# RWKV and GDN elementwise steps moved from VectorE to ScalarE in a one-core hybrid block

## The chip, the cores and the metric

The kernel runs on one core of a Trainium2 chip (TensorE, VectorE, ScalarE, GpSimd, the SyncE queue and 16 DMA engines). The metric is the device time of one execution in microseconds; the time of a kernel is the median of its runs. In the profile the engines are PE (TensorE's matmuls), PEld (its weight loads), DVE (VectorE), ACT (ScalarE), POOL (GpSimd) and SP (SyncE).

## The reference

One layer of a diffusion backbone, on 256 latent tokens and 256 context tokens of width 2048, all in float32. Each token is normalised and modulated, projected by `w_in`, and the result is cut into four head groups of width 512: GLA, Gated DeltaNet (GDN), a short gated convolution and RWKV-7. The outputs are concatenated, projected by `w_out` and added to the stream; then a SwiGLU of width 5632 and a last norm follow. The two recurrences that the change touches are:

```
GDN, per head, chunked:   S <- a (I - beta k k^T) S + beta k v^T,   o = S^T q
RWKV-7, per head, step:   S <- S (diag(w) - kk (a kk)^T) + v k^T,   y = S r
```

Every recurrent mixer runs forward and backward. The context tokens are processed first and only for their final states; each latent scan starts from the context state of its own direction.

## The kernel before

Channels lie on the 128 partitions and tokens on the free axis. Weights come from HBM in tiles `wraw` of 128x512; each is split into a high part `wh` (a copy to fp32r on ACT) and a low part `wl` (the difference, on DVE), and a product is made of three fp32r matmuls (`big` in the mixing part, `acc` elsewhere). The parts in order of time are: the modulation vectors and the first projections; the mixing part, in which projections, RWKV, GDN and GLA of context and latent tokens are interleaved; the output projection; the SwiGLU.

In the mixing part two streams run side by side. Stream "a" is RWKV (`rwkv(p, s)`: head pair p of 4, s = 0 for context and 1 for latent tokens, two directions d each), and stream "b" is GDN (`gdn(h, s)`: head h of 4, both directions and both halves of the tokens together) and GLA. The accumulation tiles of the streams lie in PSUM under the tags `ea` and `eb` (short use) and `la` and `lb` (the chains); `ea` and `big` have two buffers, the others one. Each of the pieces is traced in three parts, `front`, `mid` and `back`. The order of the pieces is written out in `ORDER`, with an offset of priority for many of them; the order of the instructions on each engine's queue is then drawn up when the program is built, from these priorities and a planner's costs of the instructions, and each engine works through its queue in that order. Loads and splits of weights have high priority.

RWKV: `front` computes `rw_BK` (two blocks of 128x256) and the tile `bdLM`, from which `small_inverses` starts its long row of small DVE steps. `mid` writes the blocks of `rw_BK` into block-diagonal tiles NB and KB (`halves`, four copies of 64x256; names `bd<-rw_BK`), and the same of v into VB on ACT; then four PE products with tiles `bd` are evicted as `rw_vt`, `rw_kt`, `rw_na` and `rw_ka`. `back` ends in a chain over four chunks: PE makes the new state and the output in one PSUM tile `la`; `rw_S` is the state, scaled by a column, and `rw_y` the output (copied on ACT for d = 0, added on DVE for d = 1).

GDN: `front` copies the product k k^T out of PSUM (`gd_kq`, line 1145) and `mid`, for latent tokens, k q^T (line 1179). In `back`, for each direction and half, PE makes `lb`, from which ACT writes `gd_Fb` (scaled by beta) and DVE writes `gd_Fg` (scaled by another column). `gd_Fg` is the stationary operand of the next product `eb`. `gd_Fb` and `gd_Fg` of one direction read the same PSUM tile, and the context tokens need 128 columns of it, the latent ones 256.

Of the kernel before, what the change touches and what calls it, by code (L numbers as in the profile page):

```python
# [175 lines left out]
def block_kernel(ctx: ExitStack, tc: tile.TileContext, x, cx, ada_first, ada_later, ada_b, w_in, w_early, w_out,  # L176
                 w_gu, w_down, final_g, consts, params, small, out):
    nc = tc.nc
    V, A, G, TE = nc.vector, nc.scalar, nc.gpsimd, nc.tensor
# [210 lines left out]
    with ExitStack() as st:  # L390
# [74 lines left out]
        w = early_weights(0)  # L465
# [50 lines left out]
    with mix:  # L516
# [382 lines left out]
        def rwkv(p, s, raw, sm):  # L899
# [52 lines left out]
            def mid(d, v):  # L952
                cur[0] = "a"
                lo = 1 if d == 0 else 0
                KK, BK = v["KK"], v["BK"]
                NB, KB, VB = (r.next() for r in bd[1:])
                vv = t1("rw_v")
                shift(vv, com["v"], d * 12 + 8 + p, d)
                halves(NB, BK[:, :, 0, :], V)
                halves(KB, BK[:, :, 1, :], V)  # L960
                halves(VB, c64(vv), A)
                if s == 1:
                    r = t1("rw_r")
                    shift(r, com["r"], d * 12 + p, d)
                    IR = v["IR"] = mk(mx, [P, 4, 2, 64], "rw_IR", 1)
                    G.tensor_copy(IR[:, :, 0, :], bcast(istack, 1, 4))
                    tt(IR[:, :, 1, :], c64(r), v["ep"][:, :, lo:lo + 64], MUL)
                    rk = t1("rw_sq")
                    stt(rk, r, pc("rk", p), v["kp"], MUL, MUL)
                    pr = PB([P, T])  # L970
                    mm(pr, onesbd, rk)
                    if d == 0:
                        com["bonus"] = t1("rw_bonus")
                        tt(com["bonus"], pr, vv, MUL)
                    else:
                        tt(rk, pr, vv, MUL)
                        tt(com["bonus"], com["bonus"], rk, ADD, e=G)

                pv = PB([P, 4, P])
                for c in range(4):  # L980
                    TE.transpose(pv[:, c], f2(VB[:, c]), ident)
                v["vt"] = mk(mx, [P, 4, P], "rw_vt", 1)
                acopy(v["vt"], pv)

                pk = PB([P, 4, P])
                for c in range(4):
                    TE.transpose(pk[:, c], f2(KK[:, c]), ident)
                v["kt"] = mk(mx, [P, 4, P], "rw_kt", 1)
                acopy(v["kt"], pk)


                for t, tag in ((NB, "rw_na"), (KB, "rw_ka")):
                    pt, o = PB([P, 4, P]), mk(mx, [P, 4, P], tag, 1)
                    for c in range(4):
                        if s == 1:
                            mm(pt[:, c], f2(t[:, c]), f2(v["IR"][:, c]))
                        else:
                            TE.transpose(pt[:, c], f2(t[:, c]), ident)
                    if s == 1:
                        tt(o, pt, bcast(caus[d], 1, 4), MUL)  # L1000
                    else:
                        for hh in range(2):
                            sl = slice(64 * hh, 64 * hh + 64)
                            acopy(o[sl, :, :64], pt[sl, :, sl])
                    v[tag] = o

            def back(d, v):
                cur[0] = "a"
                w = P if s == 1 else 64
                LM, na, ka, kt_, vt = v["LM"], v["rw_na"], v["rw_ka"], v["kt"], v["vt"]  # L1010
                KH, EB = bdKh.next(), bdE.next()
                if s == 1 and d == 0:
                    com["y"] = t1("rw_y")
                F = mk(mx, [P, 4, P], "rw_F", 1)
                inverse(v["nL"], v["Xc"], (16, 32), [d == 0] * 4, na[:, :, :w], F[:, :, :w], w)
                pka = PB([P, 4, w], "l")
                for c in range(4):
                    mm(pka[:, c], LM[:, c, 1].rearrange("p h j -> p (h j)"), F[:, c, :w])
                for hh in range(2):
                    sl = slice(64 * hh, 64 * hh + 64)  # L1020
                    tt(KH[sl, :, hh, :], pka[sl, :, 0:64], ka[sl, :, 0:64], ADD)
                if s == 1:
                    Ah = mk(mx, [P, 4, 64], "rw_Ah", 1)
                    tt(Ah, pka[:, :, 64:P], ka[:, :, 64:P], ADD)
                pe = PB([P, 4, w], "l")
                for c in range(4):
                    mm(pe[:, c], kt_[:, c], F[:, c, :w])
                for hh in range(2):
                    sl = slice(64 * hh, 64 * hh + 64)
                    tt(EB[sl, :, hh, :], pe[sl, :, 0:64], bcast(istack[sl], 1, 4), ADD)  # L1030
                if s == 1:
                    Q = mk(mx, [P, 4, 64], "rw_Q", 1)
                    tt(Q, pe[:, :, 64:P], v["IR"][:, :, 1, :], ADD)
                S = get_state(("rw", p, d), f"rw_S{d}") if s == 1 else None
                order = (0, 1, 2, 3) if d == 0 else (3, 2, 1, 0)
                yc = c64(com["y"]) if s == 1 else None
                for n, c in enumerate(order):

                    pc_ = PB([P, 64 + P], "l")
                    po, pS = pc_[:, :64], pc_[:, 64:]  # L1040
                    if n < 3 or s == 0:
                        mm(pS, f2(KH[:, c]), vt[:, c], True, S is None)
                        if S is not None:
                            mm(pS, f2(EB[:, c]), S, False, True)
                    if s == 1:
                        mm(po, vt[:, c], Ah[:, c], True, False)
                        mm(po, S, Q[:, c], False, True)
                    if n < 3 or s == 0:
                        S = mk(mx, [P, P], f"rw_S{d}", 2)
                        ts(S, pS, v["dcol"][:, c:c + 1], MUL)  # L1050
                    if s == 1 and d == 0:
                        acopy(yc[:, c], po)
                    elif s == 1:
                        tt(yc[:, c], yc[:, c], po, ADD)
                if s == 0:
                    put_state(("rw", p, d), S)
                elif d == 1:
                    finale()
# [23 lines left out]
            for d in range(2):  # L1082
                v = {}
# [13 lines left out]
        def gdn(h, s, raw, sm):  # L1097
# [29 lines left out]
            def front():  # L1127
                cur[0] = "b"
                com.update(raw())
                k = cvs(com["k"], 1, "gd_k")  # L1130
                v = cvs(com["v"], 2, "gd_v")
                l2(k, 1.0)
                tok = mk(mx, [P, 4, P], "gd_tok", 2)
                pt = PB([P, 4, P])
                for c in range(2):
                    TE.transpose(pt[:, c], k[:, c * P:(c + 1) * P], ident)
                    TE.transpose(pt[:, 2 + c], v[:, c * P:(c + 1) * P], ident)
                acopy(tok, pt)
                pk = PB([P, 2, P])
                for c in range(2):  # L1140
                    sl = slice(c * P, (c + 1) * P)
                    mm(pk[:, c], k[:, sl], k[:, sl])
                kq = mk(mx, [P, 4, P], "gd_kq", 1)
                kk = kq[:, 0:2]
                V.tensor_copy(kk, pk)

                pbc = decays()
                dl = mk(mx, [P, 4, P], "gd_dl", 2)
                for d in range(2):
                    for c in range(2):  # L1150
                        cs = sm["cum"][:, d, h, c:c + 1]
                        V.scalar_tensor_tensor(out=dl[:, d * 2 + c], in0=pbc[:, d, c * P:(c + 1) * P], scalar=cs,
                                               in1=dlm[d], op0=SUB, op1=SUB)
                act(dl, dl, AF.Exp, scale=-1.0)
                for d in range(2):
                    for c in range(2):
                        u = d * 2 + c
                        stt(dl[:, u], kk[:, c], sm["nb"][:, d, h, c:c + 1], dl[:, u], MUL, MUL)
                com.update(kq=kq, kn=k, tok=tok, nL=dl, Xc=small_inverses(dl, lowers))

            def mid():
# [14 lines left out]
                    sl = slice(c * P, (c + 1) * P)  # L1176
                    mm(pk[:, c], k[:, sl], q[:, sl])
                kq = com["kq"][:, 2:4]
                V.tensor_copy(kq, pk)
                pbc = decays()  # L1180
                for d in range(2):
                    for c in range(2):
# [9 lines left out]
            def back():  # L1192
# [7 lines left out]
                for d in range(2):  # L1200
# [5 lines left out]
                    for c in range(2):  # L1206
                        u = d * 2 + c
                        src = pf[:, c].rearrange("p a b -> p (a b)")[:, :w]
                        acopy(Fb[:, u].rearrange("p a b -> p (a b)")[:, :w], src, scale=sm["beta"][:, d, h, c:c + 1])
                        ts(Fg[:, u].rearrange("p a b -> p (a b)")[:, :w], src, sm["nbe"][:, d, h, c:c + 1], MUL)  # L1210
                    pe = PB([P, 2, 2, P])
                    for c in range(2):
                        u = d * 2 + c
# [467 lines left out]
```

## Time and profile before

| quantity | value |
|---|---|
| median of 3 runs (lowest, highest) | 1978.37 us (1975.06, 1981.58) |
| the profiled execution's own time | 1979.17 us |
| its span, first to last instruction | 1977.4 us |
| mean granted TensorE clock | 0.983 |
| PE busy in the span | 1858.0 us (94%) |
| PEld busy | 1622.9 us (82%) |
| DVE busy | 1352.5 us (68%) |
| ACT busy | 1020.7 us (52%) |
| POOL busy | 155.0 us (8%) |

The shares are averages over parts with different limits. The mixing part goes from about 160 to 1096 us of the span, and only there do the changed lines run.

### The profile page before, as it was taken

What the parts mean: (1) busy time and instruction counts of PE and PEld (TensorE: products, weight loads), DVE (VectorE), ACT (ScalarE), POOL (GpSimd) and SP (SyncE); (2) the same over time, 40 slices, a digit from 0 to 9 for tenths busy, and PEclk for the clock granted to TensorE, in tenths of its full rate; (3) what the DMA queues carried; (4) which work ended last, traced back from release to release, by engine and by line L of the source; (5) the groups of instructions that cost most, each with busy time, mean ns of one, the idle gap of its engine ahead of it and who ended that gap; (6) DMA issues with size and microseconds to landing.
All of it is one profiled execution on the core that took longest, in us unless ns stands there. A gap on an engine that the chain in (4) does not pass through costs nothing.

```text
span 1977.4 us, 36172 instructions
## 1 busy us (share of the span) xinstructions
PE 1858.0 (94%) x13312; PEld 1622.9 (82%) x13312; DVE 1352.5 (68%) x3327; ACT 1020.7 (52%) x2125; POOL 155.0 (8%) x207
## 2 busy tenths in 40 slices
PE   5898899899999999999999998999999999999998
PEld 3777788788888988888999986888888888888886
DVE  3446767888879789899767567986555555555554
ACT  2225555575575655656455555555555545544444
POOL 0001000000001001101010001110010010000000
PEclk6999999899999999999999999999999999999999
DMA  8985877255473431322344665996555555665664
GB/s 332 397 341 199 277 244 238 69 190 176 126 240 106 146 100 61 101 72 86 110 142 143 220 185 173 318 316 212 184 189 184 189 185 187 201 207 193 193 196 153
DMA packets 162081, 374.66 MB, mean 189 GB/s; under 512 B 17896, under 2 KB 43752, under 8 KB 156784
## 3 DMA queue, kind: packets, MB, share of 16 engines
q1 hardware_dynamic: 156288, 368.21, 55.7%
q10 hardware_dynamic: 5616, 4.14, 0.7%
q8 instruction: 104, 1.70, 0.3%
q14 instruction: 73, 0.60, 0.1%
HBM read 360.48 MB, written 11.80 MB: 188 GB/s over the span
## 4 chain that ended last, share of the span: by engine, by line
PE 75%; DVE 9%; DMA 8%; ACT 5%; issue 2%; POOL 0%; SPq 0%; ACTq 0%; DVEq 0%; POOLq 0%
PE acc L214 40%; PE big L214 14%; PE la L214 6%; DMA wraw<-in_ada_later 5%; PE ea L214 5%; PE lb L214 3%; DVE wl L202 3%; PE eb L214 3%; PE ob L214 2%; ACT wh L197 2%; PE pt L214 0%; DMA wraw<-in_x 0%; DMA xin<-in_cx 0%; ACT rw_z L193 0%; DMA wraw<-in_w_in 0%
## 5 line engine op out<-in xcount | busy, mean ns | idle before, releaser
L202 DVE TENSOR_TENSOR wl<-wraw,wh 128x512 fp32r<-128x512 f32 x856 | 570.7, 693 | 370.0 <-ACT wh L197 364.0
L197 ACT ACTIVATE wh<-wraw 128x512 fp32r<-128x512 f32 x856 | 509.9, 625 | 485.9 <-PE acc L214 197.0
L214 PE MATMUL acc<-n,wh 128*128 128x512 f32 x1408 | 492.7, 398 | 3.3 <-ACT wh L197 3.3
L214 PE MATMUL acc<-n,wl 128*128 128x256 f32 x1408 | 383.2, 282 | 1.8 <-DVE wl L202 1.8
L214 PE MATMUL big<-nh,wh 128*128 128x256 f32 x1056 | 311.9, 296 | 4.4 <-ACT xs L197 3.0
L214 PE MATMUL big<-nh,wl 128*128 128x256 f32 x1056 | 311.2, 295 | 0.7 <-DVE wl L202 0.7
L214 PEld LDWEIGHTS acc<-n,wh 128*128 128x128 f32 x1408 | 259.4, 189 | 60.1 <-ACT wh L197 3.6
L214 PE MATMUL big<-nl,wh 128*128 128x256 f32 x1056 | 307.7, 292 | 0.0
L214 PEld LDWEIGHTS acc<-n,wl 128*128 128x128 f32 x1408 | 267.1, 190 | 11.7 <-DVE wl L202 3.3
L214 PEld LDWEIGHTS big<-nh,wh 128*128 128x128 f32 x1056 | 200.9, 190 | 11.3 <-ACT xs L197 3.8
L214 PEld LDWEIGHTS big<-nh,wl 128*128 128x128 f32 x1056 | 200.5, 190 | 4.0 <-issue 2.1
L214 PEld LDWEIGHTS big<-nl,wh 128*128 128x128 f32 x1056 | 200.8, 190 | 2.0 <-issue 1.1
L214 PE MATMUL acc<-wh,hH 128*128 128x512 f32 x352 | 137.6, 391 | 0.0
L214 PE MATMUL acc<-wh,hL 128*128 128x512 f32 x352 | 137.2, 390 | 0.0
L214 PE MATMUL acc<-wl,hH 128*128 128x512 f32 x352 | 137.2, 390 | 0.0
L202 POOL TENSOR_TENSOR hL<-sg,hH 128x256 fp32r<-128x256 f32 x44 | 46.7, 1061 | 452.5 <-ACT hH L197 452.5
L214 PEld LDWEIGHTS acc<-wh,hH 128*128 128x128 f32 x352 | 66.1, 188 | 14.1 <-ACT up L197 0.2
L214 PEld LDWEIGHTS acc<-wl,hH 128*128 128x128 f32 x352 | 66.1, 188 | 13.9 <-DVE wl L202 0.2
L214 PEld LDWEIGHTS acc<-wh,hL 128*128 128x128 f32 x352 | 66.1, 188 | 13.8
L214 PE MATMUL ob<-wraw,sc 128*32 128x128 f32 x1536 | 52.7, 280 | 24.9 <-DMA wraw<-in_ada_later 21.2
L214 PEld LDWEIGHTS ob<-wraw,sc 128*32 128x32 f32 x1536 | 39.9, 111 | 34.2 <-DMA wraw<-in_ada_later 27.6
L202 DVE TENSOR_TENSOR wl<-wr,wh 128x1408 fp32r<-128x1408 f32 x16 | 26.0, 1624 | 43.3 <-ACT wh L197 43.3
(482 smaller groups left out, 3175.3 us busy)
## 6 DMA issues: line engine op xcount, KB each, us to landing
wraw<-in_w_gu SPq DMA_DIRECT2D x174, 512.0 KB, 3.3
wraw<-in_w_in SPq DMA_DIRECT2D x264, 256.0 KB, 3.2
wraw<-in_ada_later SPq DMA_DIRECT2D x256, 256.0 KB, 4.2
wraw<-in_w_down SPq DMA_DIRECT2D x88, 512.0 KB, 4.2
ad<-in_ada_first SPq DMA_DIRECT2D x32, 1024.0 KB, 9.8
wraw<-in_w_out SPq DMA_DIRECT2D x64, 256.0 KB, 2.8
wr<-in_w_early SPq DMA_DIRECT2D x16, 704.0 KB, 6.2
xin<-in_cx SPq DMA_DIRECT2D x2, 1024.0 KB, 7.9
```

Of the source, the lines that this page charges most:

```text
L197: A.activation(o, i, AF.Copy)
L202: (e or V).tensor_tensor(out=o, in0=a, in1=b, op=op)
L214: return TE.matmul(o, l, r, start=start, stop=stop)
```

## The change

Five sets of instructions keep their operands and results and change their engine, from DVE to ACT: RWKV's copies into NB and KB, its chunk states `rw_S`, GDN's two copies out of PSUM, and its products `gd_Fg`. `V.tensor_copy` and `ts` run on DVE; `acopy` is an ACT activation "Copy", with a scale if one is given.

```diff
@@ rwkv, mid
-                halves(NB, BK[:, :, 0, :], V)
-                halves(KB, BK[:, :, 1, :], V)
+                halves(NB, BK[:, :, 0, :], A)
+                halves(KB, BK[:, :, 1, :], A)
                 halves(VB, c64(vv), A)
@@ rwkv, back
                         S = mk(mx, [P, P], f"rw_S{d}", 2)
-                        ts(S, pS, v["dcol"][:, c:c + 1], MUL)
+                        acopy(S, pS, scale=v["dcol"][:, c:c + 1])
@@ gdn, front
-                V.tensor_copy(kk, pk)
+                acopy(kk, pk)
@@ gdn, mid
-                V.tensor_copy(kq, pk)
+                acopy(kq, pk)
@@ gdn, back
                         acopy(Fb[:, u].rearrange("p a b -> p (a b)")[:, :w], src, scale=sm["beta"][:, d, h, c:c + 1])
-                        ts(Fg[:, u].rearrange("p a b -> p (a b)")[:, :w], src, sm["nbe"][:, d, h, c:c + 1], MUL)
+                        acopy(Fg[:, u].rearrange("p a b -> p (a b)")[:, :w], src, scale=sm["nbe"][:, d, h, c:c + 1])
```

## Rows read from the trace of the kernel before

**Rows 1.** Busy time by stretch (us, instructions), granted clock, DMA share, GB/s.

```profile
core 0: us, PE busy (x) PEld busy (x) DVE busy (x) ACT busy (x) POOL busy (x), PEclk, DMA share, GB/s
...
160.00:360.00 200.00, 173.74 (x1928) 154.04 (x1928) 142.02 (x445) 113.61 (x261) 18.47 (x37) 0.98 0.75 242
360.00:960.00 600.00, 566.09 (x4729) 515.73 (x4729) 521.30 (x1658) 355.93 (x796) 52.09 (x82) 0.99 0.38 121
960.00:1096.00 136.00, 131.46 (x1022) 124.24 (x1022) 91.72 (x204) 72.98 (x159) 13.94 (x14) 1.00 0.46 146
```

**Rows 2.** What PE waited for, 360 to 960 us: total, times, longest.

```profile
PE ob L214 <- DMA wraw<-in_ada_later: 6.5, 7, 1.9
PE ea L214 <- DVE rw_BK L202: 3.9, 4, 1.3
PE eb L214 <- DVE gd_Fg L206: 3.0, 4, 1.4
...
PE ea L998 <- ACT rw_na L197: 1.8, 3, 1.2
...
PE la L214 <- DVE rw_Ah L202: 0.2, 1, 0.2
PE la L214 <- ACT ivaX L197: 0.2, 1, 0.2
```

**Rows 3.** Groups on DVE by shape: count, busy us, mean ns, idle before.

```profile
L206 DVE TENSOR_SCALAR rw_S<-la,rw_dcol 128x128 f32<-128x128 f32 x56 | 19.4, 347 | 9.3 <-PE la L214 8.8
...
L873 DVE COPY bd<-rw_BK 64x256 f32<-64x256 f32 x64 | 18.4, 287 | 1.4 <-PE ea L998 0.6
...
L206 DVE TENSOR_SCALAR gd_Fg<-lb,gnbe 128x256 f32<-128x256 f32 x16 | 7.7, 480 | 2.3 <-ACT gd_Fb L199 2.1
...
L206 DVE TENSOR_SCALAR gd_Fg<-lb,gnbe 128x128 f32<-128x128 f32 x16 | 5.5, 345 | 1.4 <-ACT gd_Fb L199 1.4
...
L1145 DVE COPY gd_kq<-eb 128x256 f32<-128x256 f32 x8 | 3.4, 419 | 0.4 <-PE eb L214 0.3
```

**Rows 4.** Groups on ACT of the nearest shapes.

```profile
L197 ACT ACTIVATE xs<-big 128x256 f32<-128x256 f32 x56 | 20.2, 371 | 0.9 <-PE big L214 0.7
...
L197 ACT ACTIVATE bd<-rw_v 64x256 f32<-64x256 f32 x32 | 13.2, 412 | 2.2 <-PE ea L981 1.6 <-DVE rw_v L211 0.2
...
L199 ACT ACTIVATE gd_Fb<-lb,gbeta 128x256 f32<-128x256 f32 x16 | 7.5, 472 | 11.3 <-PE lb L214 9.7 <-DVE gd_Fg L206 1.5
...
L199 ACT ACTIVATE gd_Fb<-lb,gbeta 128x128 f32<-128x128 f32 x16 | 5.8, 361 | 3.2 <-PE lb L214 2.3 <-DVE gd_Fg L206 0.8
```

**Rows 5.** DVE busy on rw_S, 360 to 960 us.

```profile
360.00:960.00 600.00, 15.58 (x45) 0.99 0.38 121
```

**Rows 6.** DVE busy on line 873, 360 to 960 us.

```profile
360.00:960.00 600.00, 14.37 (x50) 0.99 0.38 121
```

**Rows 7.** DVE busy on gd_Fg, 360 to 960 us.

```profile
360.00:960.00 600.00, 9.90 (x24) 0.99 0.38 121
```

**Rows 8.** Timeline of DVE: start, us, instruction.

```profile
735.40 0.28 DVE L873 COPY bd<-rw_BK 64x256 f32<-64x256 f32 x1
735.60 1.40 DVE L202 TENSOR_TENSOR bdLM<-ea,consts 64x512 f32<-64x512 f32 x2
736.92 0.89 DVE L873 COPY bd<-rw_BK 64x256 f32<-64x256 f32 x3
...
738.34 0.69 DVE L202 TENSOR_TENSOR ivaXT<-la,rw_na 128x512 f32<-128x512 f32 x1
```

**Rows 9.** Timeline of PE: the first product that reads those copies.

```profile
748.81 1.11 PE L214 MATMUL ea<-rw_IR,bd 128*128 128x128 f32 x8
```

**Rows 10.** Timeline, 952 to 957 us: one direction of GDN's products.

```profile
952.19 0.47 ACT L199 ACTIVATE gd_Fb<-lb,gbeta 128x256 f32<-128x256 f32 x1 [1.22 <-PE lb L214]
952.69 0.48 DVE L206 TENSOR_SCALAR gd_Fg<-lb,gnbe 128x256 f32<-128x256 f32 x1
953.21 0.47 ACT L199 ACTIVATE gd_Fb<-lb,gbeta 128x256 f32<-128x256 f32 x1 [0.55 <-DVE gd_Fg L206]
...
953.72 0.48 DVE L206 TENSOR_SCALAR gd_Fg<-lb,gnbe 128x256 f32<-128x256 f32 x1 [0.54 <-ACT gd_Fb L199]
```

**Rows 11.** What ACT waited for, 360 to 960 us, longest first.

```profile
ACT wh L197 <- PE big L214: 36.4, 41, 2.8
```

**Rows 12.** What DVE waited for, 360 to 960 us, longest first.

```profile
DVE wl L202 <- ACT wh L197: 10.2, 20, 1.5
```

## Prediction

> **What bounds the kernel now.** I read the table of busy shares first. PE is busy for 94% of the span, so a change of elementwise work can only act through what PE still waits for, and all changed lines lie in the mixing part. I therefore read the busy time of three stretches of that part [rows 1]. From 160 to 360 us PE is idle for 200 - 173.7 = 26.3 us; from 360 to 960 us for 600 - 566.1 = 33.9 us; from 960 to 1096 us for 136 - 131.5 = 4.5 us. That is 64.7 us in all, and no rearrangement can give back more. The middle stretch is the one to look at: there DVE is busy for 521.3 of 600 us (86.9%) and ACT for 355.9 us (59.3%). In the first stretch DVE is at 71% and the DMA engines at 75% of their time, so I expect little from DVE there.
>
> Next I read what PE waited for in the middle stretch [rows 2]. The list has 24 lines and names 32.2 of the 33.9 us. One line of 6.5 us is DMA. Sixteen lines are DVE: the first is 3.9 us, the last 0.2 us, and they sum to 19.1 us. Seven are ACT: from 1.8 us down to 0.2 us, sum 6.6 us. So the stalls that DVE ends are three times those that ACT ends. PE is the bound, with DVE close behind.
>
> **The change part by part.** Each moved instruction has its price on DVE in its own row [rows 3], and its price on ACT in that of an ACT instruction of the same shape and the same kind of source [rows 4].
>
> *Off DVE:* 56 states, 19.4 us; 64 block copies, 18.4 us; 32 `gd_Fg`, 7.7 + 5.5 = 13.2 us; eight copies of line 1145, 3.4 us; four of line 1179, which have the same shape, at 419 ns, 1.7 us. Sum 56.1 us.
>
> *Onto ACT:* the states are priced as `gd_Fb` of 128x128 (also scaled by a column, also out of PSUM): 56 x 361 ns = 20.2 us. The block copies are priced as ACT's own copies into the third of these tiles, `bd<-rw_v`: 64 x 412 ns = 26.4 us. `gd_Fg` is priced as its twin `gd_Fb`: 16 x 472 + 16 x 361 ns = 13.3 us. The 12 copies out of PSUM are priced as `xs<-big`: 12 x 371 ns = 4.5 us. Sum 64.4 us. The sources of the block copies are strided here and not in the row; the other rows of 256 columns bound it by 371 and 472 ns, 23.7 to 30.2 us, and I keep 412 since the destination is the same.
>
> So the engines' work grows by 8.3 us, nearly all of it from the block copies (287 ns on DVE against 412 on ACT). The Trainium skill ("Perfetto Trace Analysis", section "Optimizing Scalar/DVE Operations") says that an operation for which DVE has a fast mode is quicker there, and that offloading to ACT may make sense if DVE is saturated. By it the block copies should stay, and without them the sums would be 37.7 us off DVE and 38.0 us onto ACT.
>
> In the middle stretch the moved work is 15.6 us of states, 14.4 us of block copies and 9.9 us of `gd_Fg` [rows 5 to 7], 39.9 us together, and most of the 5.1 us of small copies; I take 43 us. DVE falls to 478 of 600 us (79.7%). ACT gains 43 x 64.4 / 56.1 = 49 us and rises to 405 us (67.6%).
>
> *What a lighter DVE is worth.* One place shows it [rows 8]: of four block copies in DVE's queue one stands ahead of `bdLM` and three, 0.89 us, stand ahead of `ivaXT` at 738.34 us, which PE needs. The first product that reads them starts at 748.81 us [rows 9], more than 10 us after the last ends. The copies themselves are therefore hidden behind the rest of the stream, and stay so on ACT unless they come more than 10 us later; what they cost now is the place that they take in the queue. How much of the 19.1 us of stalls goes away with 43 us less in that queue no row shows, so I bound it. If stalls go with busy time, it is 19.1 x 43/521 = 1.6 us less, and on the side of ACT 6.6 x 49/356 = 0.9 us more: net gain 0.7 us. If they go as in a queue, with u/(1-u) of the busy share u, DVE's factor falls from 6.63 to 3.93 (to 59%) and ACT's rises from 1.46 to 2.09 (to 143%): 7.8 us less and 2.8 us more, net gain 5.0 us. I take 3 us, between them.
>
> *The GDN pair.* `gd_Fb` and `gd_Fg` of one direction never overlap [rows 10]: ACT and DVE take turns on one PSUM tile, four turns from 952.19 to 954.20 us, though the four durations sum to 1.90 us, and each turn waits for the other engine's queue. On one engine the turns need no handover, so the four ACT products can take about 4 x 0.47 = 1.88 us. I give this 1 us of the 3.0 us that PE lost to `gd_Fg` [rows 2]; the bounds are 0 (if other ACT work is put between) and 3.0 us.
>
> *The states.* In a forward chunk `rw_S` and `rw_y` now follow one another on ACT and lose a handover between engines; in a backward chunk `rw_y` stays on DVE and gains one. There are as many of one kind as of the other, and `rw_S` costs 14 ns more on ACT, 56 x 14 ns = 0.8 us. I cost this at nothing; what hides it is the `big` matmuls that PE has between chunks, and without them it is 0.8 us.
>
> *Who queues behind.* Behind every moved instruction on ACT stand the copies `wh`, then DVE's `wl` and PE's projections. ACT sat idle 36.4 us before `wh`, in 41 places, because PE had not yet released a buffer [rows 11], so `wh` is mostly early; but DVE already waits 10.2 us for it, 20 times [rows 12]. That is cover for delays of some tenths of a microsecond each, not for all 49 us.
>
> Sum: 3 + 1 = 4 us less. The profiled execution took 1979.2 us, 0.8 us more than the median of the runs; so 1975.2 on its scale and 1974.4 as a median. I predict 1974.5 us.
>
> **The rivals.**
>
> *DVE sets the pace of the middle stretch.* DVE's 521.3 us is more than the weight loads' 515.7 us [rows 1], and work that PE needs queues behind copies that nobody needs yet. If so, nearly all of DVE's 19.1 us goes; ACT's share comes back a little. Price 15 us: 1963.5 us, and 1959 with all 19.1. Against it: PE at 94% leaves no more, and DMA and ACT own 13.1 us of the idle time. The Trainium skill ("Perfetto Trace Analysis", section "Identifying the Most-Contended Engine") would rate DVE as the engine to relieve, since it judges PE by its weight loads; by that rule this rival would be the forecast.
>
> *ACT comes late in RWKV's `mid` (slower).* Four copies of 412 ns, 1.65 us, now stand in ACT's queue near `rw_vt`, `rw_kt`, `rw_na` and `rw_ka`, whose evictions free the two `ea` buffers; PE already waited there for `rw_na` [rows 2]. There are 64/4 = 16 such places: 26.4 us if none is covered. With half uncovered it is 13 us, less 4 us gained: +9 us, 1987.5 us. It decides once the stalls that ACT ends grow by over 10 us. Against it: the 10 us of slack of the copies, which allows them to be queued after the evictions.
>
> *The queues are drawn up anew and fit less well.* New durations and engines change the order of every queue in the mixing part. No row prices it. The nearest are the idle shares of PE in the stretches, 13% in the first, 5.7% in the second and 3.3% in the third [rows 1]: one point more in 600 us is 6 us, and a third of the way from 5.7 to 13% is +14 us, 1992 us. It may as well go the other way by half of that.
>
> *Nothing moves:* what PE waits for is the length of the chains, and a freed DVE only waits longer. 1978 us.
>
> **How the numbers follow.** Chances: forecast 0.43 (its own range, from the bounds, 1969 to 1980 us); DVE sets the pace 0.22; ACT late 0.17; queues fit less well 0.13; nothing moves 0.05. The runs of before spread over 0.33%, so 0.3% (5.9 us) is what can be told from no change: faster is below 1972.4 us, slower above 1984.3. Faster: the second case, 0.22, and the lower third of the first, 0.14, give 0.36. Slower: 0.17 and 0.13, 0.30. Same: 0.34. The range has to reach both the DVE case, whose bound is 1959 us, and a poor order of the queues: 1958 to 1995 us.
>
> **What would show it.** DVE's busy time should fall from 1352.5 to about 1296 us and ACT's rise from 1020.7 to about 1085 us, with PE's at about 1858. PE's stalls that DVE ends should fall from 19 to about 14 us in the stretch that answers to 360 to 960 us, and those of ACT rise from 7 to about 9. `gd_Fb` and `gd_Fg` should stand four in a row on ACT. I am wrong on the gain if PE's idle time in that stretch stays at 34 us, and wrong on the sign if stalls behind `wh`, `rw_kt` or `rw_na` grow by more than 10 us, or if PE's stalls turn up at lines that the change doesn't touch.

## The result and the profile after

The change makes the kernel slower: 1987.56 us against 1974.46 us, medians of 11 runs each, taken in turn on one chip; the ratio is 1.0055, with a 95% interval of 1.0039 to 1.0071. The forecast was 4 us less. It started from 1978.37 us, the median of three runs; with eleven runs the kernel before has 1974.46 us, so it is the step of -4 us, and not the number 1974.5, that the result answers. The time lies inside the range given, on the other side of "no change".

The first view of the profile after is the busy time by stretch, in the columns of [rows 1].

```profile
160.00:360.00 200.00, 172.47 (x1910) 152.72 (x1910) 129.85 (x409) 119.91 (x283) 18.47 (x37) 0.97 0.75 241
360.00:960.00 600.00, 565.61 (x4708) 510.34 (x4709) 493.02 (x1537) 401.94 (x931) 56.68 (x86) 1.00 0.38 120
960.00:1096.00 136.00, 130.27 (x1000) 123.18 (x999) 88.69 (x190) 73.92 (x164) 11.44 (x10) 0.99 0.44 140
```

The work did change sides: in the middle stretch DVE fell from 521.3 to 493.0 us and ACT rose from 355.9 to 401.9 us [rows 1]. PE gained nothing from it: it is busy for 565.6 of 600 us, as before (566.1), and does fewer matmuls in the same time: 18, 21 and 22 fewer in the three stretches, 61 in all. At the 7.8 matmuls per us of the middle stretch (4708 in 600 us) that is a lag of some 8 us, an estimate, of the 9.7 us by which the profiled execution is longer (span 1987.1 against 1977.4 us).

The second view is what PE waited for in the middle stretch, in the columns of [rows 2], the first and some later ones of its 28 lines.

```profile
PE ea L214 <- DVE rw_BK L202: 7.7, 7, 2.8
...
PE la L718 <- DVE ivaX L202: 1.6, 3, 1.0
...
PE la L214 <- ACT ivaW L197: 1.1, 2, 0.6
...
PE la L214 <- ACT rw_S L199: 0.7, 2, 0.5
```

All lines of it sum to 32.8 us, against 32.2 us before. Those that DVE ends fell from 19.1 to 16.9 us (14 was forecast), those that ACT ends rose from 6.6 to 9.4 us (9 was forecast). `gd_Fg`, 3.0 us before [rows 2], is not in the list any more; the wait for `rw_BK` has grown from 3.9 to 7.7 us, though nothing that makes `rw_BK` was changed.

The prices, by groups on ACT, in the columns of [rows 4]:

```profile
L197 ACT ACTIVATE bd<-rw_BK 64x256 f32<-64x256 f32 x64 | 26.5, 414 | 10.2 <-DVE rw_BK L211 9.3 <-DVE rw_BK L202 0.2
L199 ACT ACTIVATE rw_S<-la,rw_dcol 128x128 f32<-128x128 f32 x56 | 20.5, 366 | 25.9 <-PE la L214 25.4
L199 ACT ACTIVATE gd_Fg<-lb,gnbe 128x256 f32<-128x256 f32 x16 | 7.6, 473 | 0.0
L199 ACT ACTIVATE gd_Fg<-lb,gnbe 128x128 f32<-128x128 f32 x16 | 5.9, 370 | 0.0
L197 ACT ACTIVATE gd_kq<-eb 128x256 f32<-128x256 f32 x12 | 4.6, 381 | 2.8 <-PE eb L214 2.7
```

They sum to 65.1 us (64.4 was forecast), and every single price is within 10 ns of its forecast. One direction of GDN's products, in the timeline of ACT that answers to [rows 10], stands as foreseen, four in a row with 0.36 to 0.37 us from start to start (0.50 to 0.52 before):

```profile
943.52 0.47 ACT L199 ACTIVATE gd_Fb<-lb,gbeta 128x256 f32<-128x256 f32 x1 [0.32 <-PE lb L214]
943.89 0.47 ACT L199 ACTIVATE gd_Fg<-lb,gnbe 128x256 f32<-128x256 f32 x1
944.25 0.47 ACT L199 ACTIVATE gd_Fb<-lb,gbeta 128x256 f32<-128x256 f32 x1
944.61 0.48 ACT L199 ACTIVATE gd_Fg<-lb,gnbe 128x256 f32<-128x256 f32 x1
```

What stands behind ACT did get later: the line of [rows 12], DVE's wait for `wh` in the middle stretch, has nearly doubled.

```profile
DVE wl L202 <- ACT wh L197: 19.4, 21, 2.9
```

PE did not pay for that: it waited 0.7 us for `wl` in this stretch before and after, and 1.4 and 1.0 us for `wh`.

So the prices were right and the pair was right, and the time went the other way. The experiments ask for the reason.

### The profile page after: what moved, and what is told of

Read it like the earlier page. It is cut to its first block, busy times and chain, and to the rows that moved or that the text cites. A ratio compares the mean times of both kernels' runs of the same rounds, so it can differ in the third digit from the quotient of the medians.

```text
span 1987.1 us, 36206 instructions
## 1 busy us (share of the span) xinstructions
PE 1863.5 (94%) x13311; PEld 1622.2 (82%) x13312; DVE 1314.4 (66%) x3163; ACT 1076.4 (54%) x2289; POOL 155.9 (8%) x207
## 3 DMA queue, kind: packets, MB, share of 16 engines
q1 hardware_dynamic: 156288, 368.21, 55.7%
## 4 chain that ended last, share of the span: by engine, by line
PE 72%; DVE 10%; DMA 8%; ACT 6%; issue 2%; POOL 1%; SPq 0%; ACTq 0%; DVEq 0%; POOLq 0%
PE acc L214 39%; PE big L214 13%; PE la L214 6%; DMA wraw<-in_ada_later 6%; PE ea L214 5%; PE lb L214 4%; DVE wl L202 3%; PE eb L214 2%; PE ob L214 2%; ACT wh L197 2%; DMA wraw<-in_w_in 1%; DVE ivaw L202 1%; ACT rw_z L193 0%; PE pt L214 0%; DVE ivaXc L202 0%
## 6 DMA issues: line engine op xcount, KB each, us to landing
ad<-in_ada_first SPq DMA_DIRECT2D x32, 1024.0 KB, 10.2
```

## Experiments

Two things happen at once when an instruction changes its engine: its duration and neighbours change, and, since the program draws up the queues when it is built, the order of every queue in the mixing part changes with it. Between the kernels before and after, 3722 lines of PE's queue differ. The first set of experiments holds one of the two fixed. A function called after the kernel's body chains the instructions of each engine in a recorded order, by dependencies that order without a semaphore:

```diff
         block_kernel(tc, *aps, o)
+        _pin(tc, nc)
...
+        if e in last:
+            tc.add_manual_dep(ins, last[e], info, reason="pin")
+        last[e] = ins.name
```

"Old order" below is that of the kernel before, in which a moved instruction stands in ACT's queue at the place that the order of the whole program gives it; "new order" is that of the kernel after. All ratios are to the kernel before, timed beside it on the same chip in five rounds.

### e1 and e2: engines and order apart

e1 has the four parts of the change and the old order; e2 has none of them and the new order.

> The moved instructions run on ACT as in the change, but every queue keeps the order that it had before (each moved instruction stands on ACT where it stood in the old overall order). Theory order (the loss of 0.55% comes from the queues being drawn up anew): ratio 0.995 to 1.001, since only the lighter DVE and the GDN pair are left. Theory engines (ACT, with some 55 us more, comes late): ratio 1.003 to 1.010 here too, with PE's stalls ended by ACT up by over 8 us.

> The reverse: all work on the engines that it had before, but every queue in the order of the changed kernel. Theory order: ratio 1.004 to 1.010, as slow as the change or slower. Theory engines: 0.998 to 1.002, as the kernel before.

e1 took 1985.04 us, ratio 1.0057 (1.0039 to 1.0076); e2 took 2011.18 us, ratio 1.0194 (1.0174 to 1.0215). The engines alone, with every instruction of PE in its old place, lose as much as the whole change. The new order alone loses over three times as much; it was drawn for the new engines, and the likely reason, not tested by itself, is that it fits the old ones badly. The waits of PE in e1, 160 to 1110 us:

```profile
PE eb L214 <- ACT gd_Fg L199: 6.2, 9, 1.4
PE ea L214 <- DVE rw_BK L202: 4.0, 6, 1.3
...
PE eb L214 <- DVE ivbR L202: 2.0, 2, 1.4
PE la L214 <- DVE ivaXc L202: 2.0, 2, 1.2
PE la L214 <- ACT ivaW L197: 1.9, 3, 1.1
PE ea L998 <- ACT rw_na L197: 1.8, 4, 0.9
PE la L214 <- DVE ivaXT L202: 1.6, 1, 1.6
PE la L214 <- DVE rw_y L202: 1.5, 2, 1.2
```

In the kernel before, the same view over the same time has `rw_BK` 4.3, `ivbR` 2.0, `ivaXc` 2.0, `ivaXT` 1.4 and `rw_y` 1.5 us. These are DVE's largest besides `gd_Fg`, and with 38 us less work on DVE they are the same to 0.3 us. What grew is what ACT ends: `gd_Fg` from 3.0 us, on DVE, to 6.2 us, and `ivaW` from 0.4 to 1.9 us. All that ACT ends went from 16.2 to 24.3 us, up by 8.1 us, as theory "engines" expected.

Why `ivaW` grew is seen at one place, in the timeline of ACT; first the kernel before, then e1 (here some 0.6 us behind), each with the first product that reads `ivaW`, and in e1 with the first one that reads the block copies.

```profile
450.81 0.62 ACT L197 ACTIVATE ivaQ<-bdLM 32x128 f32<-32x128 f32 x2
451.46 0.39 ACT L197 ACTIVATE ivaW<-la 128x256 f32<-128x256 f32 x1
...
451.89 1.10 PE L214 MATMUL la<-ivaW,ivaL 128*128 128x64 f32 x8
```

```profile
451.33 0.41 ACT L197 ACTIVATE bd<-rw_BK 64x256 f32<-64x256 f32 x1
451.65 0.29 ACT L197 ACTIVATE ivaQ<-bdLM 32x128 f32<-32x128 f32 x1
451.95 0.42 ACT L197 ACTIVATE bd<-rw_BK 64x256 f32<-64x256 f32 x1
452.38 0.30 ACT L197 ACTIVATE ivaQ<-bdLM 32x128 f32<-32x128 f32 x1
452.71 0.41 ACT L197 ACTIVATE bd<-rw_BK 64x256 f32<-64x256 f32 x1
453.15 0.38 ACT L197 ACTIVATE ivaW<-la 128x256 f32<-128x256 f32 x1
...
453.58 1.10 PE L214 MATMUL la<-ivaW,ivaL 128*128 128x64 f32 x8 [1.10 <-ACT ivaW L197]
...
469.70 0.60 PE L998 MATMUL ea<-ident,bd 128*128 128x128 f32 x4
```

Three block copies, which no product reads for another 16 us, now stand in front of `ivaW`, which PE needs at once: 1.10 us. In e5, where the block copies alone are moved, PE waits the same 1.10 us here.

The prediction found a picture like it on DVE, three copies in front of `ivaXT` [rows 8]. There they cost PE less. First its weight load in the kernel before, then `ivaXT` at the same place in e1:

```profile
739.08 0.97 PEld L214 LDWEIGHTS la<-ivaXT,ivaX 128*128 128x128 f32 x8 [0.33 <-DVE ivaXT L202]
```

```profile
739.77 0.69 DVE L202 TENSOR_TENSOR ivaXT<-la,rw_na 128x512 f32<-128x512 f32 x1 [0.59 <-PE la L214]
```

Eight `big` products filled the time, and 0.33 us were left. In e1 the copies are gone from DVE, `ivaXT` itself waits 0.59 us for PE, and its weight load has no wait any more.

### e5 to e8: one part at a time, old order

e5 moves the block copies alone, e6 the states, e7 `gd_Fg`, e8 the small copies out of PSUM, with the edits of the change.

> Only the 64 block copies go to ACT, each where it stood in the old overall order; all queues otherwise as before. Their products come more than 10 us later, so theory pair (what costs is work that PE needs at once, moved to ACT) expects 0.996 to 1.001. Theory engines (any work added to ACT's queue delays the splits and the evictions behind it) expects 1.002 to 1.005, as the largest piece of work moved.

> Only the 56 states go to ACT, in the old order. Theory pair: 1.000 to 1.003, since the next chunk's products wait for a state. Theory engines: 1.001 to 1.004.

> Only the 32 products gd_Fg go to ACT, in the old order. Theory pair: 1.002 to 1.004, most of the loss of the whole change in this order (0.57%), because in the run with all of them PE's products of gd_Fg come 3.9 us later. Theory engines: 1.000 to 1.002, by its 13 us of 64.

> Only the twelve small copies go to ACT, with every queue kept in the old order. Theory order (the 0.58% that the same move cost with newly drawn queues is that of the queues): 0.998 to 1.002. If ACT itself is the cause: 1.004 to 1.008, as with newly drawn queues.

| part alone, old order | ratio | 95% interval |
|---|---|---|
| block copies | 1.0009 | 0.9991 to 1.0028 |
| states | 1.0014 | 0.9999 to 1.0028 |
| `gd_Fg` | 1.0018 | 1.0003 to 1.0034 |
| small copies | 1.0001 | 0.9988 to 1.0013 |

No part shows a gain. The product is 1.0042; the whole in e1 is 1.0057, and their intervals overlap. One part alone is at the edge of what can be told: only the interval of `gd_Fg` lies wholly above 1, and that no ratio lies below 1 is the reading. Between the theories "pair" and "engines" the three runs e5 to e7 don't decide, since each interval reaches into both bands. e8 also shows that the chaining itself costs nothing that can be told.

### e3 and e4: what drawing the queues anew costs

e3 moves only the small copies and lets the queues be drawn anew. e4 moves nothing and changes one offset:

```diff
-ORDER = ("rw0:-50 pd3 pd2:550 ...
+ORDER = ("rw0:-40 pd3 pd2:550 ...
```

> Only GDN's twelve small copies out of PSUM go to ACT (5 us of work); the queues are drawn up anew, and about as many lines of PE's order differ as with the whole change. Theory order: the time may move by 0.2 to 0.8% either way, though the work hardly does. Theory engines: 0.998 to 1.002.

> Nothing is moved between engines; one offset in ORDER (rw0) is -40 and not -50, which draws the queues up anew over more than half as many lines as the change. Theory order: a time off by 0.2 to 0.8% either way. Theory engines: 0.998 to 1.002.

e3: 1.0058 (1.0038 to 1.0077), against 1.0001 for the same edit in the old order; that loss is the drawing alone. e4: 1.0026 (1.0012 to 1.0039), for a step of ten in one priority. So about half the loss of the whole change can come without any moved work, and all of it with 5 us of moved work that cost nothing in the old order.

### e9, e10 and e12: the place in ACT's queue

e9 is e1, and e10 is e7, with each `gd_Fg` directly behind its `gd_Fb`. e12 is e1 with ACT's queue left to be drawn anew.

> All four parts on ACT, every queue in the old order, but each gd_Fg put on ACT directly behind its gd_Fb (in the old order one to three other ACT instructions stand between them in 24 of 32 places). Theory A, what the change loses in the old order is the place of gd_Fg behind other ACT work: PE's waits for gd_Fg between 160 and 1110 us fall from 6.2 us to under 1 us, its weight loads' from 9.0 us to under 2, and the ratio falls from 1.0057 to about 1.003 or below. Theory B, the loss is spread over the chains and turns up wherever the queues meet: the waits for gd_Fg fall but others grow, and the ratio stays between 1.0045 and 1.007.

> Only gd_Fg on ACT, every queue in the old order, but each gd_Fg directly behind its gd_Fb. The step of the prediction, two products in a row without a handover give about 1 us (0 to 3.0): ratio 0.9995, at the most 0.9985, and PE's waits for gd_Fg go from 5.1 us to under 1 us. Theory B, a stall that goes at one place comes back at the next: the waits for gd_Fg go, and the ratio stays at 1.001 to 1.002.

> All four parts on ACT; the queues of PE, DVE, GpSimd and the DMA issues in the old order, ACT's queue alone drawn up anew. If the loss in the old order (1.0057) is the place of the moved instructions in ACT's queue: 1.001 to 1.003. If it lies in the durations and chains whatever ACT's order, or in the order of PE's queue: 1.005 to 1.007. If a queue drawn for another order of PE fits worse, as with the old engines in the new order: above 1.009.

e9: 1.0045 (1.0027 to 1.0063); e10: 1.0009 (0.9993 to 1.0025); e12: 1.0123 (1.0105 to 1.0141). The first two are some 0.1% below e1 and e7, a difference within the intervals. Some of PE's waits in e9 over 160 to 1110 us follow. The second line is a product that reads `gd_Fg`, though it is put down to DVE: its weight load waits 2.74 us for `gd_Fg` of ACT, and in ACT's timeline four other instructions stand ahead of that `gd_Fb` and `gd_Fg`.

```profile
PE ea L998 <- ACT rw_na L197: 3.6, 4, 2.7
...
PE eb L214 <- DVE ivaXc L202: 2.6, 1, 2.6
...
PE eb L214 <- ACT gd_Fg L199: 0.6, 2, 0.4
```

6.2 us have become 0.6 + 2.6 us, about what `gd_Fg` cost on DVE (3.0 us), while `rw_na` has doubled from 1.8 to 3.6 us. By the waits, the place of `gd_Fg` behind other ACT work is a part of what e1 loses; in the time that part can't be told from nothing, and most of the loss is there without it, as theory B expected. e12 fell outside what any theory but the last expected: ACT's queue, drawn anew for another order of PE, costs twice as much as the old one, with 6.0 us of waits for `ivaX` (0.7 in e1) and 2.8 us for `rw_S`.

### e11, e13 to e16: the same offsets with the old and the new engines

If a drawing can lose 0.3 to 0.6%, is the whole change just one more draw? e13 has the offset rw0:-60 and e15 the offset RW0:40, both without the change; e11 (rw0:-40), e14 (rw0:-60) and e16 (RW0:40) have the whole change.

> The whole change, and the offset of rw0 in ORDER -40 instead of -50, which draws the queues anew. If the new engines cost a fixed amount and the offset another (1.0026 without the change): about 1.008. If each drawing of the queues scatters by some tenths of a per cent and the change as a whole is one more draw: anywhere from 1.000 to 1.008, and outside 1.0039 to 1.0071 more likely than not.

> Nothing moved; the offset of rw0 in ORDER is -60 instead of -50, which draws more of PE's queue anew than the whole change does (3944 against 3722 lines of difference). If the loss of the whole change is that of any new drawing of the queues: 1.003 to 1.007. If a new drawing costs nothing by itself and the new engines do: within 0.2% of 1.

> The whole change with the offset of rw0 at -60. If the loss is that of any new drawing, it is no slower than the same offset with the old engines: a difference of less than 0.2% between the two, of either sign. If the new engines cost something of their own in every order: slower than the same offset with the old engines by 0.3 to 0.5%.

> Nothing moved; the offset of RW0 is 40 instead of 50 (309 lines of difference in PE's queue). A small new drawing: if the size of the new drawing sets its cost, within 0.1% of 1; if any drawing scatters by some tenths of a per cent, up to 1.003.

> The whole change with the offset of RW0 at 40. If the new engines cost something of their own in every order: slower than the same offset with the old engines by 0.3 to 0.6%, so 1.003 to 1.007. If only the drawing counts: anywhere between 0.999 and 1.006, and no slower than the same offset with the old engines in one of the three pairs of offsets at least.

| offsets | old engines (interval) | new engines (interval) | quotient |
|---|---|---|---|
| as before | 1 | 1.0055 (1.0039 to 1.0071) | 1.0055 |
| rw0:-40 | 1.0026 (1.0012 to 1.0039), e4 | 1.0065 (1.0047 to 1.0084), e11 | 1.0039 |
| rw0:-60 | 1.0068 (1.0046 to 1.0090), e13 | 1.0108 (1.0083 to 1.0134), e14 | 1.0040 |
| RW0:40 | 1.0005 (0.9988 to 1.0021), e15 | 1.0081 (1.0060 to 1.0102), e16 | 1.0076 |

In all four the new engines are slower, by 0.39 to 0.76%, mean 0.53%. An estimate of the quotients' intervals from those of the two ratios leaves each above 1, for rw0:-60 only just (1.0006 to 1.0074). The drawing scatters over 0.68% by itself, and the order of the kernel before is the best of its four; but the loss is not only that. Nor is the scatter even to both sides: the more lines of PE's queue a drawing changes, the more it loses (309 lines in e15, 1.0005; more than half of 3722 in e4, 1.0026; 3944 in e13, 1.0068), as if the offsets of the kernel before had been chosen for its engines. Whether other offsets, searched for the new engines, would be faster than the kernel before is not tested.

The side of ACT shows in all four pairs too. The waits of PE's weight loads that ACT ends, 160 to 1110 us, are 36.7, 30.6, 39.1 and 29.6 us with the old engines and 44.2, 44.0, 53.7 and 43.6 us with the new ones, in the order of the table: 7.5 to 14.6 us more. Those that DVE ends change by +3.2, -4.2, -10.4 and +2.8 us, so a lighter DVE doesn't lower them reliably. Now the waits of PE in e13, 160 to 1110 us, nothing moved:

```profile
PE ea L214 <- DVE rw_BK L202: 8.2, 8, 1.6
PE lb L214 <- DVE ivbW L202: 5.1, 7, 1.4
```

The kernel after has 8.4 and 2.6 us in these lines over the same time, the kernel before 4.3 and 0.6 us. So the stalls "at lines that the change doesn't touch" are a matter of the order: the long waits for `rw_BK` come with some drawings without any moved work (e13: 8.2 us, but e15: 3.7 us), with all four of the new engines (6.9 to 8.8 us), and in the old order they stay away (e1: 4.0 us).

## Why the prediction was wrong

**What bounds the kernel: right.** PE is busy for 94% of the span before and after, and its idle time in the middle stretch stayed at 34 us (600 - 565.6 = 34.4), the sign that the prediction named against its gain.

**The step that failed: what a lighter DVE is worth** (3 us, bounds 0.7 and 5.0). Both bounds let DVE's stalls shrink with its busy share, by 1.6 to 7.8 us. In e1 PE's order is that of before, and DVE's share in the middle stretch falls from 521.3 to 491.1 us. The stalls of PE that DVE ends there fall from 19.1 to 15.9 us, but 3.0 us of that are the line of `gd_Fg`, which only changed its engine: 0.2 us were given back. The weight loads, where these stalls show longer (1.31 us for `ivaW` at the place above, 1.10 us at the product), give the same reading over 160 to 1110 us; these are lines before, then in e1:

```profile
PEld eb L214 <- DVE gd_Fg L206: 4.4, 7, 1.6
PEld la L214 <- ACT ivaW L197: 1.7, 6, 0.6
```

```profile
PEld eb L214 <- ACT gd_Fg L199: 9.2, 14, 1.6
PEld la L214 <- ACT ivaW L197: 3.3, 6, 1.3
```

The sums of all lines, before and in e1, are: ended by DVE 26.2 and 20.8 us, by ACT 36.7 and 52.5 us, by all releasers 122.7 and 131.8 us. Of the 5.4 us that DVE lost, 4.4 us are `gd_Fg`. So a DVE that is lighter by 38 us gave back 1.0 us, and ACT took 15.8 us, of which `gd_Fg` is 9.2 us, the rest `ivaW` (+1.6), the states (1.6, a line that was not there) and smaller ones. Even the 1.0 us can't be told from nothing: without `gd_Fg` DVE's sum lies between 20.6 and 23.9 us in the kernel before and the seven runs that hold every queue (e1, e5 to e10). (The section on the kernel before calls `gd_Fg` the stationary operand of its product. In the code it is the second operand, which streams through with 128 or 256 columns; the weight load of that product waits for it all the same.)

The trace of the kernel before had the answer to the question that the prediction bounded. Between 160 and 1110 us PE waited 31 times for DVE besides `gd_Fg`, 20.5 us. DVE's timeline has moved work inside the wait, or in the 2 us ahead of it, at five of them, for 0.8 us at most. At the others DVE was, where it was busy, at work that stayed: at the steps that lead to the awaited one, or, as here, at a `wl` in front of it.

```profile
444.10 0.69 DVE L202 TENSOR_TENSOR wl<-wraw,wh 128x512 fp32r<-128x512 f32 x1
444.70 0.65 DVE L202 TENSOR_TENSOR ivbR<-ivbd,consts 128x480 f32<-128x480 f32 x1
...
445.50 1.04 PE L214 MATMUL eb<-ivbR,consts 128*128 128x480 f32 x2 [1.43 <-DVE ivbR L202]
```

**The side of ACT** (0.9 to 2.8 us in the same sum) was mis-sized with it: 8.1 us more at the matmuls (16.2 to 24.3 us) and 15.8 us at the weight loads. A busy share of 59% said that there was room; what counted is that single moved instructions stand directly in front of, or behind, an instruction that PE waits for. The cover named for it, `wh` early by 36.4 us [rows 11], did not hold for `wl`: DVE's wait for `wh` went from 10.2 us [rows 12] to 19.4 us. But PE's own waits for `wh` and `wl` did not grow, so that is not where the time went.

**The prices: right** in each, but not as sums of busy time: DVE fell by 38.1 us (1352.5 to 1314.4) and not 56.1 us, and ACT rose by 55.7 us (1020.7 to 1076.4) and not 64.4 us, because durations of neighbours in a queue overlap, as the starts in [rows 8] show (0.28 us long, the next 0.20 us later).

**The GDN pair: right in its mechanism.** In the kernel after the four stand in a row and PE's 3.0 us for `gd_Fg` are gone. That needs the row: in the old order, where other ACT work stands between, they become 6.2 us (the lower bound, nothing, was too kind by 3.2 us), and e10 against e7 shows the worth of the row as 0.09%, which can't be told from nothing.

**The states at nothing: open.** e6 has 1.0014 (0.9999 to 1.0028), which can't be told from nothing; but the weight loads wait for `rw_S` for 1.6 us in e1 and 3.3 us in the kernel after, a line that was not there before.

**The rivals.** "ACT comes late in RWKV's mid" had the sign, and a price (9 us) near the 10.9 us that 0.55% are; its place was wrong, so the price was luck. In e1 PE waits for `rw_na` and `rw_kt` as long as before (1.8 and 0.7 against 1.8 and 0.6 us), and the block copies alone cost 0.09%; the copies delay `ivaW`, and ACT's other delays are mostly GDN's and the states'. "The queues fit less well" had its size right for a drawing as such: 14 us were forecast, and e13 lost 0.68% of 1975.5 us, 13.4 us. For this change it isn't needed to explain a loss of this size, since e1 loses as much without it. "Nothing moves" had the side of DVE right, a freed DVE that only waits longer, and not the side of ACT. "DVE sets the pace" is refuted by e1 and e9, where DVE has 38 and 36 us less to do and the kernel is slower. The Trainium skill ("Perfetto Trace Analysis", section "Identifying the Most-Contended Engine") would optimise the busiest engine first and judges PE by its weight loads; in the middle stretch that engine was DVE, and relieving it gained nothing here. The section "Optimizing Scalar/DVE Operations" of that page of the Trainium skill expects operations with a fast mode on DVE to be quicker there; the block copies were (287 ns on DVE, 414 on ACT), though no row shows in which mode DVE ran them.

**What stays open.** The loss of the kernel after can't be split line by line between engines and drawing: its queue on PE is another one, and the sums differ from one drawing to the next. Part of it is not idle time at all: of the 9.7 us by which the profiled execution of after is longer, 4.2 us are idle time of PE and 5.5 us are busy time (1858.0 to 1863.5 us) for the same matmuls, and no run shows why. Nor do single profiled executions carry tenths of a per cent: e8, whose ratio is 1.0001, has a span of 1971.5 us, 5.9 us less than the profiled execution of before. That the loss is the same 0.55% with the old and with the new order is thus not shown to have one cause. No version tried beats the kernel before.

## What to carry to other kernels

A stall that an engine ends is not a stall that a lighter engine ends sooner: before moving work for the sake of a busy share, look at each wait in the list whether the work to be moved runs on that engine during it or just ahead of it (here at 5 of 31 waits, 0.8 of 20.5 us), and on the new engine look for what the moved instruction will stand in front of. Where queues are drawn up by the program, time the same edit in the old order, and some arbitrary redrawings without the edit; here the latter alone moved the time by up to 0.68%. A change of a few tenths of a per cent is judged only against that spread.

## What the runs showed of the hardware

Two products from one PSUM tile start 0.36 us apart when both are ACT's, and 0.50 to 0.52 us apart when ACT and DVE take turns, although each takes 0.47 to 0.48 us on either engine; what the pair gains is the overlap of neighbours in one queue and the handover. For a 128x256 copy out of PSUM ACT was the quicker one (381 ns against 419 on DVE), for a 128x128 product by a column DVE (347 ns against 366).
